# Turning part of the second stage's input with VectorE and DRAM instead of TensorE

## The chip, the cores and the metric

The kernel runs on one core of a Trainium2 chip. The metric is the device time of one execution in microseconds (us). The time before the change is the median of three runs.

## What is computed

The reference is a decoder trunk of two layers over 512 tokens and a model width of 2048, all in float32. The first layer is differential attention. Its normalised output is the input of the second stage: a shared projection to keys, values and forget gates, and then the second layer, forgetting attention. Cut to what matters here:

```python
x  = layer_norm(DN_ALPHA * x + gate * y, ln_g[0], ln_b[0])      # end of layer 0; (512, 2048)
hk = x * (1.0 + scale) + shift                                   # scale and shift per feature
k, v, zf = split(hk @ w_kv)                                      # shared keys, values, gate logits
...
h  = x * (1.0 + scale_b) + shift_b                               # the second layer's own modulation
q, g = split(h @ w_q)
```

## The kernel before

A product of float32 matrices is made of three matmuls: each operand is split into a high part, rounded to the type that TensorE reads fast, and a low part, the rest. TensorE multiplies high by high, high by low and low by high (`products`, L174 to L176). Weights come by DMA into `wst` (four buffers, L76), ScalarE makes the high part `whi` (L94) and VectorE the low part `wlo` (L95), with three buffers each.

TensorE contracts over partitions, so the activations `Hh` and `Hl` have features on partitions and tokens along the row: 16 tiles of 128 features by 512 tokens. The layer norm needs the other layout. Its result `n` is one tile of 128 partitions with four row blocks b of 128 tokens, each 2048 features wide; `norm_a(b)` writes it (the first 1024 features by ScalarE, L1072; the rest by VectorE, L1073) and stores it to `n_dram` for later use (L1074). It runs when row block b has been through the last quarter of the first layer's output projection, so block 3 is ready last.

`build_half(s, half)`, L1076 to L1097, turns one unit: features 256 s to 256 s + 255 (two tiles, kt = 2s and 2s + 1) of the tokens 256 half to 256 half + 255 (two row blocks). TensorE makes four transposes of 128x128 through the identity into a PSUM bank (L1084). For each of the two tiles ScalarE applies scale and shift twice, to `htmp2` in float32 (L1092) and to the high part `Hh` (L1093), and VectorE subtracts for the low part `Hl` (L1094). Last, VectorE copies the turned tokens back into the place of `n` that they came from (L1097); from there `build_h` (L1118 to L1124) makes the second layer's `Hh` and `Hl` some 250 us later, one VectorE instruction of 512 columns for each of 16 tiles and a split.

There are 16 units. The loop at L1188 uses them in the order of `lag`:

```python
lag = [(0, 0), (0, 1), (0, 2), (0, 3), (1, 0), (1, 1), (1, 2)]
for s in range(4, KT // 2):
    lag += [(0, s), (1, s - 1)]
lag.append((1, KT // 2 - 1))
```

Each entry is (half, s). An iteration makes the first 512 value columns for the two row blocks of its half and the two tiles of its s: twelve matmuls of 512 columns. Two units are built ahead of the loop, in the tail of the output projection; every iteration but the third builds the next one, so the unit of iteration i + 1 is built in iteration i. The weights of one s serve both halves and stay in `held` in between; those of s = 3 lie in a tile of another pool, the others in the three buffers of `whi` and `wlo`.

All DMAs that the change touches are issued by SyncE (SP), whose queue also loads the weights (L47). The tile framework orders each engine's instructions by a simulated schedule, in which an instruction traced later may go first when its inputs are ready; `keep_in_program_order` holds one behind the instruction traced before it on its engine. In this loop the background stream that sums the modulation vectors (L393) does not run.

The kernel already turns other tiles by a trip through DRAM: the attention weights of both layers and the first layer's output (L760 and L768, L826 and L834, L1302 and L1310). A VectorE instruction turns every 32x32 block in itself, one DMA writes the result to DRAM, and four or eight DMAs of 32 partitions each read the blocks back in their new places.

## Time and profile before

| | |
|---|---|
| median of three runs | 1961.45 us (1961.02 to 1962.36) |
| the profiled execution | 1958.95 us |
| its span | 1957.2 us |
| mean granted TensorE clock over the span | 0.995 |
| busy: TensorE (PE), its weight loads, VectorE, ScalarE | 98%, 83%, 69%, 36% |
| transposes of n (L1084) | 64, from 983.3 to 1034.9 us |

Times in the profile are microseconds from the start of the span unless marked ns. PE is TensorE's matmul, PEld its weight load, DVE is VectorE, ACT ScalarE, SP the engine that issues most DMAs; a q behind a name is that engine's instruction sequencer. A line of the timeline has the start, the duration, the engine, the line of the kernel, the operation and what it writes and reads; x2 or x4 at its end says that it stands for so many instructions; in brackets is the idle time ahead of it and what ended that. A line of the stretches has the stretch, its length, the busy time of PE, PEld, DVE, ACT and POOL with their counts, the granted clock of TensorE as a share of full speed, the busy share of the DMA engines and GB/s.

### The profile page before, as it was taken

The numbers are of one execution on the slowest core, as the hardware profiler recorded it, in microseconds if no ns is written. First come the engines' busy times: TensorE is split into PE (matmuls) and PEld (weight loads), VectorE is DVE, ScalarE is ACT, GpSimd is POOL, SyncE is SP. The second block draws the span as 40 slices with busy tenths as digits, with TensorE's granted clock in tenths as the row PEclk, the third lists the DMA queues.
The fourth block names the chain that finished last, engine by engine and source line by source line (L and its number), as shares of the span: only waits on it lengthen the run. The fifth ranks groups of instructions, "written<-read, shape, count | busy, mean of one in ns | idle before, by whom it ended". The sixth has DMA issues, their size and how long they took to land.

```text
span 1957.2 us, 25652 instructions
## 1 busy us (share of the span) xinstructions
PE 1923.4 (98%) x8997; PEld 1619.0 (83%) x8997; DVE 1355.0 (69%) x2499; ACT 700.0 (36%) x1186; POOL 2.2 (0%) x10
## 2 busy tenths in 40 slices
PE   5999999999999999999999999999999999999997
PEld 4888888888888888888889998888888888888886
DVE  7886578767777778567675657776566666676657
ACT  2432444323332344531273223224343434353123
POOL 0000000000000000000000000000000000000000
PEclk8999999999999999999999999999999999999999
DMA  9983355676667675466537866775354555553622
GB/s 343 361 302 118 124 183 166 202 229 204 213 203 224 190 238 177 130 229 214 181 133 233 270 202 215 245 260 163 110 157 148 153 154 153 156 173 113 223 91 104
DMA packets 337582, 376.16 MB, mean 192 GB/s; under 512 B 67974, under 2 KB 247196, under 8 KB 336684
## 3 DMA queue, kind: packets, MB, share of 16 engines
q1 hardware_dynamic: 334496, 370.30, 58.8%
q10 hardware_dynamic: 2956, 4.22, 0.6%
q8 instruction: 71, 1.16, 0.2%
q14 instruction: 59, 0.48, 0.1%
HBM read 345.63 MB, written 28.79 MB: 191 GB/s over the span
## 4 chain that ended last, share of the span: by engine, by line
PE 93%; DVE 3%; DMA 1%; SPq 1%; issue 1%; ACT 0%; DVEq 0%; ACTq 0%
PE acc L174 28%; PE acc L175 28%; PE acc L176 28%; PE sc L174 2%; PE sc L175 2%; PE sc L176 2%; PE o L174 1%; PE o L175 1%; PE o L176 1%; DVE wlo L95 1%; SPq L473 0%; PE tr L541 0%; DMA nr<-n_dram 0%; DMA wst<-in_a_w_in_dram 0%; DVE sacc L500 0%
## 5 line engine op out<-in xcount | busy, mean ns | idle before, releaser
L94 ACT CAST whi<-wst 128x1024 fp32r<-128x1024 f32 (+3 forms) x330 | 333.5, 1011 | 736.5 <-PE acc L176 339.5
L95 DVE TENSOR_TENSOR wlo<-wst,whi 128x1024 fp32r<-128x1024 f32 (+3 forms) x330 | 385.7, 1171 | 280.6 <-ACT whi L94 267.9
L174 PE MATMUL acc<-whi,hh 128*128 128x512 f32 (+1 forms) x1296 | 494.0, 384 | 1.0 <-DVE ztmp L1007 1.0
L175 PE MATMUL acc<-wlo,hh 128*128 128x512 f32 (+1 forms) x1296 | 492.4, 380 | 0.3 <-DVE wlo L95 0.3
L176 PE MATMUL acc<-whi,hl 128*128 128x512 f32 (+1 forms) x1296 | 491.8, 380 | 0.0
L174 PE MATMUL acc<-hh,whi 128*128 128x512 f32 x1184 | 463.6, 392 | 0.0
L175 PE MATMUL acc<-hl,whi 128*128 128x512 f32 x1184 | 461.7, 390 | 0.0
L176 PE MATMUL acc<-hh,wlo 128*128 128x512 f32 x1184 | 460.9, 390 | 0.0
L174 PEld LDWEIGHTS acc<-whi,hh 128*128 128x128 f32 x1296 | 244.5, 189 | 41.0 <-DVE ztmp L1007 1.8
L176 PEld LDWEIGHTS acc<-whi,hl 128*128 128x128 f32 x1296 | 243.2, 188 | 41.7
L175 PEld LDWEIGHTS acc<-wlo,hh 128*128 128x128 f32 x1296 | 243.4, 188 | 38.9 <-DVE wlo L95 0.7
L393 DVE SCALAR_TENSOR_TENSOR macc<-ms,cact,macc 128x512 f32<-128x512 f32 x307 | 229.2, 747 | 56.3 <-DMA ms<-in_w_mod_dram 38.4
L176 PEld LDWEIGHTS acc<-hh,wlo 128*128 128x128 f32 x1184 | 222.3, 188 | 47.7
L174 PEld LDWEIGHTS acc<-hh,whi 128*128 128x128 f32 x1184 | 222.5, 188 | 43.2 <-issue 0.3
L175 PEld LDWEIGHTS acc<-hl,whi 128*128 128x128 f32 x1184 | 222.5, 188 | 42.2
L500 DVE SCALAR_TENSOR_TENSOR sacc<-sms,cact,sacc 128x512 f32<-128x512 f32 (+1 forms) x127 | 89.5, 705 | 5.7 <-DMA sms<-in_w_mod_dram 2.0
L728 ACT ACTIVATE e<-e,mn 128x128 f32<-128x128 f32 (+3 forms) x64 | 36.0, 563 | 103.0 <-DVE mn L724 102.9
L1289 ACT ACTIVATE eb<-eb,mnb 128x128 f32<-128x128 f32 (+1 forms) x64 | 36.0, 563 | 88.8 <-DVE mnb L1286 88.6
L724 DVE CUSTOM_DVE_ANT_0 e<-sc,bias 128x128 f32<-128x128 f32 (+3 forms) x64 | 31.1, 486 | 25.2 <-PE sc L176 25.2
L1286 DVE CUSTOM_DVE_ANT_0 eb<-sc,biasb 128x128 f32<-128x128 f32 (+1 forms) x64 | 31.1, 486 | 23.0 <-PE sc L176 22.4
L393 DVE SCALAR_TENSOR_TENSOR macc<-msk,cact,macc 128x512 f32<-128x512 f32 x53 | 39.7, 749 | 1.0
L1280 DVE SCALAR_TENSOR_TENSOR biasb<-nfb,F,mask 128x128 f32<-128x128 f32 (+1 forms) x64 | 34.6, 542 | 0.6
(264 smaller groups left out, 1714.9 us busy)
## 6 DMA issues: line engine op xcount, KB each, us to landing
wst<-in_a_w_in_dram SPq DMA_DIRECT2D x240, 256.0 KB, 3.8
ms<-in_w_mod_dram SPq DMA_DIRECT2D x136, 256.0 KB, 3.8
ms<-in_kv_w_mod_dram SPq DMA_DIRECT2D x64, 512.0 KB, 4.4
wst<-in_b_w_in_dram SPq DMA_DIRECT2D x128, 256.0 KB, 2.8
sms<-in_w_mod_dram SPq DMA_DIRECT2D x56, 512.0 KB, 6.8
wst<-in_kv_w_dram SPq DMA_DIRECT2D x40, 512.0 KB, 3.8
ms<-in_w_mod_dram SPq DMA_DIRECT2D x32, 512.0 KB, 4.2
wst<-in_a_w_out_dram SPq DMA_DIRECT2D x32, 512.0 KB, 4.2
```

Source lines behind the costliest of these rows:

```text
L94: self.nc.scalar.copy(hi[:, :, :w], st[:, :, :w])
L95: self.nc.vector.tensor_tensor(lo[:, :, :w], st[:, :, :w], hi[:, :, :w].bitcast(F32), op=ALU.subtract)
L174: PE.matmul(dst, lhs[0], rhs[0], start=start, stop=False)
L175: PE.matmul(dst, lhs[0], rhs[1], start=False, stop=False)
L176: PE.matmul(dst, lhs[1], rhs[0], start=False, stop=stop)
L393: ins = V.scalar_tensor_tensor(acc, w, cact[:, kt : kt + 1], acc, op0=ALU.mult, op1=ALU.add)
L500: V.scalar_tensor_tensor(acc, w, sc, acc, op0=ALU.mult, op1=ALU.add)
L724: V.tensor_tensor_reduce(out=e[:, :w], in0=sc[:, :w], in1=st["bias"][:, (3 - i) * P :], scale=-1.0, scalar=3.0e38, op0=ALU.add, op1=ALU.mi ...
L728: S.activation(e[:, :w], e[:, :w], AF.Exp, bias=mn, scale=-1.0, accum_out=rs)
L1280: V.scalar_tensor_tensor(bias[:, :w], cur[hd, "nf"][:, :w], F[:, i, hd : hd + 1], mask[:, (3 - i) * P :], op0=ALU.add, op1=ALU.add)
L1286: V.tensor_tensor_reduce(out=e[:, :w], in0=sc[:, :w], in1=bias[:, :w], scale=-1.0, scalar=3.0e38, op0=ALU.add, op1=ALU.min, accum_out=mn)
L1289: S.activation(e[:, :w], e[:, :w], AF.Exp, bias=mn, scale=-1.0, accum_out=rs)
```

## The change

Twelve of the 16 units are no longer turned by TensorE: all eight of half 1, and s = 4 to 7 of half 0. They go in six pairs (s, s + 1). `turn_n` has VectorE turn the 32x32 blocks of a pair with four instructions of 256 columns into a tile `tn` (two buffers), each pinned behind the VectorE instruction traced before it, and one DMA writes the 512 KB to a DRAM tile (three buffers). `fetch_n` reads them back with eight DMAs of 32 partitions, in pieces of 256 bytes, over the place in `n` that they came from. `turns` and `back` say in which iteration of the loop either happens: the pair (s 0 and 1, half 1) is turned in iteration 0, fetched in iteration 1 and built in iterations 3 and 4.

For a turned unit `build_half` has no transposes, no PSUM bank and no copy back. ScalarE reads the fetched `n` in SBUF instead; a row block of it now holds one tile's 256 tokens with its 32-token groups interleaved, and the access pattern of `place_n` puts them in order. `build_h` reads the same pattern, in two instructions of 256 columns for each tile instead of one of 512.

```diff
+    turned_n = {}
+    def turn_n(s, half):
+        pool, n, _ = zp
+        t = pool.tile([P, 2, 2, 256], F32, name="tn", tag="tn", bufs=2)
+        for u in range(2):
+            for q in range(2):
+                c0 = (2 * (s + u) + q) * P
+                src = n[:, 2 * half : 2 * half + 2, c0 : c0 + P].rearrange("p b (j c) -> p b j c", c=32)
+                tc.keep_in_program_order(V.transpose(t[:, q, u, :].rearrange("p (j b c) -> p b j c", b=2, c=32), src))
+        turned_n[s, half] = turned_n[s + 1, half] = dram.tile([2, 2, P, 256], F32, name="turned_n", tag="turned_n", bufs=3)
+        nc.sync.dma_start(turned_n[s, half].rearrange("q u p e -> p q u e"), t)
+
+    def fetch_n(s, half):
+        src = turned_n[s, half].rearrange("q u (a r) (j e) -> q j r (u a) e", a=4, j=4)
+        for j in range(4):
+            for q in range(2):
+                to = zp[1][32 * j : 32 * j + 32, 2 * half + q, 2 * s * P : (2 * s + 4) * P]
+                nc.sync.dma_start(to.rearrange("p (x e) -> p x e", e=64), src[q, j])
+
+    def place_n(s, half, q):
+        return zp[1][:, 2 * half + q, 2 * s * P : (2 * s + 2) * P].rearrange("p (a b c) -> p b a c", b=2, c=32)

     def build_half(s, half):
         pool, n, _ = zp
+        hs = slice(256 * half, 256 * half + 256)
+        if turned(s, half):
+            for q in range(2):
+                kt = 2 * s + q
+                if half == 0:
+                    new_h(kt)
+                tmp = pool.tile([P, 256], F32, name="htmp2", tag="htmp2", bufs=2)
+                src = place_n(s, half, q)
+                sc, sh = ab["kv"][0][:, kt : kt + 1], ab["kv"][1][:, kt : kt + 1]
+                for dst in (tmp, Hh[kt][:, hs]):
+                    S.activation(dst.rearrange("p (b a c) -> p b a c", b=2, c=32), src, AF.Identity, scale=sc, bias=sh)
+                V.tensor_tensor(Hl[kt][:, hs], tmp, Hh[kt][:, hs].bitcast(F32), op=ALU.subtract)
+            return
         px = sc_bank()
...
     def build_h(kts, ab):
...
-            nt = n[:, :, kt * P : (kt + 1) * P]
-            V.tensor_scalar(tmp.rearrange("p (b t) -> p b t", t=P), nt, ab[0][:, kt : kt + 1], ab[1][:, kt : kt + 1], op0=ALU.mult, op1=ALU.add)
+            s, q = divmod(kt, 2)
+            for half in range(2):
+                to = tmp[:, 256 * half : 256 * half + 256]
+                if turned(s, half):
+                    to, nt = to.rearrange("p (b a c) -> p b a c", b=2, c=32), place_n(s, half, q)
+                else:
+                    to, nt = to.rearrange("p (b t) -> p b t", t=P), n[:, 2 * half : 2 * half + 2, kt * P : (kt + 1) * P]
+                V.tensor_scalar(to, nt, ab[0][:, kt : kt + 1], ab[1][:, kt : kt + 1], op0=ALU.mult, op1=ALU.add)
...
+    turns = {0: (0, 1), 1: (2, 1), 2: (4, 0), 3: (6, 0), 5: (4, 1), 8: (6, 1)}
+    back = {1: (0, 1), 2: (2, 1), 3: (4, 0), 5: (6, 0), 7: (4, 1), 10: (6, 1)}
     for i, (half, s) in enumerate(lag):
+        if i in back:
+            fetch_n(*back[i])
+        if i in turns:
+            turn_n(*turns[i])
         if i != 2:
             build_next()
```

More of the change, by code (lines that the diff above doesn't have):

```diff
@@ L1074, in norm_a, with turned @@
         nc.sync.dma_start(n_dram[b * P : (b + 1) * P, :], n[:, b, :])
+    turned_n = {}
[15 more added lines that the diff above has]
+                nc.sync.dma_start(to.rearrange("p (x e) -> p x e", e=64), src[q, j])
+    def turned(s, half):
+        return (s, half) in turned_n
+    def place_n(s, half, q):
+        return zp[1][:, 2 * half + q, 2 * s * P : (2 * s + 2) * P].rearrange("p (a b c) -> p b a c", b=2, c=32)
     def build_half(s, half):
         pool, n, _ = zp
+        hs = slice(256 * half, 256 * half + 256)
[11 more added lines that the diff above has]
+            return
         px = sc_bank()
-        hs = slice(256 * half, 256 * half + 256)
         for q in range(2):
```

## The prediction

> **What bounds the kernel now.** I read the page first, for the engine that carries the time, then the PE timeline of the stage that the change touches, then what the stage's PE work waits for.

> ```profile
> span 1957.2 us, 25652 instructions
> PE 1923.4 (98%) x8997; PEld 1619.0 (83%) x8997; DVE 1355.0 (69%) x2499; ACT 700.0 (36%) x1186; POOL 2.2 (0%) x10
> PE 93%; DVE 3%; DMA 1%; SPq 1%; issue 1%; ACT 0%; DVEq 0%; ACTq 0%
> ```

> The span is PE work from end to end: 98% busy, and 93% of the chain that ended last. So time that PE saves or loses in a stage reaches the end one for one, unless another wait takes its place. The profiled execution took 1958.95 us around this span; the median of the runs shown is 1961.45, 2.5 us above. I make the sum as a difference inside the profiled execution and add it to the median. A measurement of this kernel tells about 0.2%, 3.9 us, from no change.

> The stage is the loop over `lag`: sixteen iterations of twelve matmuls each. The PE timeline, start and duration first:

> ```profile
> 994.03 0.40 PE L174 MATMUL acc<-whi,hh 128*128 128x512 f32 x1
> ...
> 998.60 0.39 PE L176 MATMUL acc<-whi,hl 128*128 128x512 f32 x1
> 998.84 0.27 PE L1084 MATMUL sc<-ident,n 128*128 128x128 f32 x1
> ...
> 1000.15 0.55 PE L1084 MATMUL sc<-ident,n 128*128 128x128 f32 x3
> ...
> 1015.27 0.60 PE L1084 MATMUL sc<-ident,n 128*128 128x128 f32 x4
> ...
> 1018.48 0.60 PE L1084 MATMUL sc<-ident,n 128*128 128x128 f32 x4
> ```

> From 994.03 to 998.60 there are 21 matmuls, 20 steps: 0.2285 us each. An iteration without transposes is therefore 12 x 0.2285 = 2.74 us. With a unit's four transposes it is 1018.48 - 1015.27 = 3.21. So four transposes cost PE 0.47 us, not the sum of their durations.

> At 998.84 the first transpose of unit (half 1, s 0) goes out, and the other three only at 1000.15. The reason, and the end of the stage:

> ```profile
> 998.85 1.25 ACT L1072 ACTIVATE n<-n,mr,lrstd 128x1024 f32<-128x1024 f32 x1 [3.30 <-DVE mr L1071]
> PEld sc L1084 <- ACT n L1072: 0.6, 1, 0.6
> 1040.69 0.59 ACT L1139 COPY vt<-acc 128x512 f32<-128x512 f32 x1 [0.54 <-PE acc L176]
> 998.84:1040.70 41.86, 41.73 (x207) 34.05 (x206) 24.55 (x43) 31.52 (x59) 0.00 (x0) 1.00 0.26 86
> ```

> The fourth row block of n is normalised at 998.85 + 1.25 = 1000.10, by ACT. PE waits 0.6 us for it. At 1040.69 the last accumulator of the stage is read out. From 998.84, where iteration 3 begins, to there are 41.86 us with 13 iterations: 13 x 2.74 = 35.65 of products, and 6.2 of transposes and waits. That 6.2 us is all that the change can win, since units 0 to 3 keep their transposes.

> **The change part by part.**

> *Removed from PE:* 48 transposes in 12 units, 12 x 0.47 = 5.6 us; with the wait of 0.6 that is the 6.2 above, all of it on the path.

> *Vector and scalar work.* Rows of the groups by shape (count, then busy us and mean ns):

> ```profile
> L1300 DVE STREAM_TRANSPOSE tb<-eb 128x256 f32<-128x256 f32 x14 | 6.2, 444 | 0.4
> L1097 DVE COPY n<-sc 128x512 f32<-128x512 f32 x16 | 10.8, 683 | 0.0
> L1092 ACT ACTIVATE htmp<-sc,mod_b,mod_a 128x256 f32<-128x256 f32 x32 | 18.1, 565 | 5.5 <-PE sc L1084 5.1 <-DVE hl L1094 0.4
> L1123 DVE TENSOR_SCALAR htmp<-n,mod_a,mod_b 128x512 f32<-128x512 f32 x16 | 8.7, 543 | 0.3
> 1280.00:1350.00 70.00, 70.00 (x311) 57.68 (x310) 56.06 (x83) 24.50 (x32) 0.00 (x0) 1.00 0.62 208
> ```

> 24 VectorE transposes of 256 columns come in, 24 x 0.444 = 10.7 us; 12 copies go out, 12 x 0.683 = 8.2. DVE gains 2.5 us in a stage where it works 24.6 of 41.9: hidden under PE. ACT's 48 activations keep shape and number, at 565 ns, and now read SBUF. In `build_h` each 512-column instruction becomes two of 256: at most 16 x 0.543 = 8.7 us more, if halves cost as much as wholes, in a stretch where DVE works 56.1 of 70 and PE is busy all 70. Hidden too; with that cover gone it would cost those 8.7.

> *The trip through DRAM.* Per pair of units: one write of 512 KB, and eight reads of 64 KB on the same SP queue. A read waits on SP for the write to land, and behind it are queued the next write and the weight loads (L47); the loads run stages ahead. The rows (KB, then median us from issue to landing), and SP's timeline:

> ```profile
> n_dram<-n SPq DMA_DIRECT2D x4, 1024.0 KB, 4.3
> turned<-tb SPq DMA_DIRECT2D x14, 256.0 KB, 2.0
> turned<-e SPq DMA_DIRECT2D x5, 256.0 KB, 4.5
> pTl<-turned SPq DMA_DIRECT2D x56, 64.0 KB, 2.2
> e<-turned SPq DMA_DIRECT2D x20, 64.0 KB, 4.6
> 785.71 3.86 SPq L834 DMA_DIRECT2D ogT<-turned_og  x8
> 1000.12 0.34 SPq L1074 DMA_DIRECT2D n_dram<-n  x1
> ```

> The first pair is (half 1, s 0 and 1), needed by iteration 4, the one after the 998.84 iteration. Its clock starts at 1000.10, because each transpose reads row blocks 2 and 3 together, and the pinned order puts it behind the norm:

> 1. Four transposes, 4 x 0.444 = 1.8: 1001.9.
> 2. The write. Bounds 2.0 and 4.5, by the two 256 KB rows. I take 4.0, near the upper, because the 1 MB store of n goes out at 1000.12 on the same queue ahead of it, and by its own 4.3 lands at 1004.4; the reads overwrite n and must wait for that store as well. 1005.9.
> 3. The reads. Eight issues in 3.86 us are about 0.49 apart. The activations of q = 0 need the seventh: 6 x 0.49 = 2.9, 1008.8. Landing between 2.2 and 4.6; I take 2.2, from the calmer stage, as the background stream does not run here: 1011.0.
> 4. Two activations, the second making the high part: by the rows below 0.47 apart and 0.56 long, 1.0: 1012.0.

> ```profile
> 1015.90 0.56 ACT L1092 ACTIVATE htmp<-sc,mod_b,mod_a 128x256 f32<-128x256 f32 x1 [0.78 <-PE sc L1084]
> 1016.37 0.56 ACT L1093 ACTIVATE hh<-sc,mod_b,mod_a 128x256 fp32r<-128x256 f32 x1
> ```

> PE's cover for this ends at 998.84 + 2.74 = 1001.6, the end of iteration 3. Nothing can be pulled forward:

> ```profile
> 1005.78 1.05 ACT L94 CAST whi<-wst 128x1024 fp32r<-128x1024 f32 x1 [0.83 <-PE acc L176]
> ```

> This cast, the weights of s = 4, waits for PE to finish with s = 0, since `whi` has three buffers; so unit (0, 4) cannot go ahead of (1, 0). PE stands from 1001.6 to 1012.0: **10.4 us** where it stood under one. With the low ends (2.0, 2.2) it is 8.4; with the high ends (4.5, 4.6) about 13.3.

> *The later pairs.* Two iterations use a pair up in 5.5 us; SP needs eight issues and a write, about 4.4. If the writes go out ahead of the waiting reads, the second pair's seventh read is issued at 1005.9 + 3.9 + 2.9 = 1012.7, in place by 1015.9 with landing and activations, and iteration 6 asks for it at 1012.0 + 5.5 = 1017.5. I cost the later pairs at nothing, covered by 1.6 us.

> *The clock after the stall.* The first 60 us show what an idle PE does to its clock (third number from the end):

> ```profile
> 30.00:32.00 2.00, 1.11 (x4) 0.71 (x4) 0.98 (x3) 0.55 (x1) 0.00 (x0) 0.56 1.10 376
> 32.00:34.00 2.00, 0.99 (x2) 0.83 (x3) 0.34 (x1) 1.63 (x3) 0.00 (x0) 0.50 1.10 376
> 34.00:36.00 2.00, 2.00 (x6) 1.58 (x5) 1.93 (x4) 0.00 (x0) 0.00 (x0) 0.50 1.09 385
> 36.00:38.00 2.00, 2.00 (x8) 1.53 (x8) 1.93 (x3) 0.71 (x1) 0.00 (x0) 0.73 1.09 385
> 44.00:46.00 2.00, 2.00 (x6) 1.52 (x6) 0.83 (x3) 0.10 (x1) 0.00 (x0) 0.50 1.08 376
> 46.00:48.00 2.00, 2.00 (x10) 1.67 (x9) 2.00 (x4) 0.60 (x1) 0.00 (x0) 0.67 1.09 385
> ```

> Twice the granted clock fell to 0.50 when PE had little to do and came back only after some us of full work. What was lost: 2 x (0.44 + 0.50 + 0.50 + 0.27) = 3.4 us in the first fall, 2 x (0.50 + 0.33) = 1.7 in the second. A stall of 10 us should do the same; bounds 1.7 and 3.4, I take 2.6, the middle, having no row nearer to either. [...]

> *The sum.* 35.65 + 10.4 + 2.6 = 48.65 us against 41.86: **+6.8 us**. From the median, 1968.3; the profiled execution would be near 1965.8. With all low ends 35.65 + 8.4 + 1.7 = 45.75, +3.9; with all high ends 35.65 + 13.3 + 3.4 = 52.35, +10.5.

> **The rivals.**

> *The trip is covered (faster).* If iteration 4 finds its input in time, the 6.2 us are won: 1955.2. The point that decides is stall plus clock loss below 6.2. For it: the scheduler sets each engine's order anew, and could bring the norm of the fourth row block forward, where ACT today waits 3.30 us for DVE. Against it: even so, with the low ends, the trip is 1.8 + 2.0 + 2.9 + 2.2 + 1.0 = 9.9 us, and the input would have to be ready near 992, 8 us earlier.

> *Short trip, clock holds (no change that can be told).* Low ends and no fall of the clock: 35.65 + 8.4 = 44.05, +2.2: 1963.6. For it: the calm rows of 2.0 and 2.2 come from a stage with traffic of its own. Against it: a gap of 8 us, and the store of n ahead in the queue.

> *SP serves pair after pair (slower still).* If a pair's write stands behind the eight reads of the pair before, each pair takes a write's landing (3.0, between 2.0 and the 4.0 taken above) and eight issues, 3.0 + 3.9 = 6.9 us, against 5.5 that PE needs: 1.4 us late for each of five pairs, 7 more, +13.8: 1975.3. For it: `fetch_n` comes before `turn_n` in every iteration, and SP works in order. Against it: SP's order is the scheduler's, which today puts another tile's write straight behind four reads:

> ```profile
> 1414.23 2.95 SPq L1310 DMA_DIRECT2D pTl<-turned  x4
> 1417.22 0.43 SPq L1302 DMA_DIRECT2D turned<-tb  x1
> ```

> **How the numbers follow.** The forecast, +3.9 to +10.5, has 0.55; the SP rival 0.17; the short trip 0.17; the covered trip 0.11. Slower by over 0.2% is 0.55 + 0.17 = 0.72; within 0.2% is 0.17; faster 0.11. The range 1962.0 to 1975.0 leaves out the covered trip and the far end of the SP rival. The likeliest case's own range is 1965.3 to 1972.0.

> **What would show it.** Right: TensorE transposes of n from 64 to 16; a PE gap of 8 to 13 us about 1002 on the old axis, ended by an ACT activation that itself waited for the fetched n; a granted clock near 0.5 for some us behind it; iterations of 2.74 us after that, with no second gap. Wrong: PE passing 1002 without a gap, or a gap under 5 us; a gap before every second iteration would mean the SP rival; PE gaps in the 1280 to 1350 stretch would mean that the split `build_h` was not free.

## The result, and the profile after

| | before | after |
|---|---|---|
| median | 1961.02 us (1960.45 to 1962.36, 5 runs) | **1981.26 us** (1980.51 to 1985.5, 5 runs) |
| ratio, 95% interval | | **1.0107 (1.0093 to 1.0122)** |
| the profiled execution, its span | 1958.95, 1957.2 | 1985.5, 1983.7 |

The change costs 20.2 us. The forecast was 6.8 slower, 1962.0 to 1975.0: the sign held, the size did not.

The top of the page of the changed kernel, to be laid beside the page of before:

```profile
span 1983.7 us, 25652 instructions
PE 1928.7 (97%) x8949; PEld 1619.4 (82%) x8949; DVE 1358.8 (68%) x2527; ACT 701.5 (35%) x1186; POOL 2.2 (0%) x10
PE 90%; DVE 4%; DMA 3%; SPq 1%; ACT 1%; issue 1%; DVEq 0%; ACTq 0%
```

PE has 48 matmuls fewer (8949 against 8997): the transposes are gone. PE holds 90% of the last chain where it held 93%, and DMA 3% where it held 1%.

How much of this is the stage? ScalarE's weight casts (L94 and L89) are the same in both kernels, so they can be counted off. The 161st lies ahead of the stage, the 201st behind it. Their rows, before and then after:

```profile
934.46 1.05 ACT L94 CAST whi<-wst 128x1024 fp32r<-128x1024 f32 x1 [4.39 <-PE acc L176]
1121.68 0.84 ACT L94 CAST whi<-wst 128x776 fp32r<-128x776 f32 x1 [3.40 <-PE acc L176]
```
```profile
936.38 1.05 ACT L94 CAST whi<-wst 128x1024 fp32r<-128x1024 f32 x1 [4.39 <-PE acc L176]
1143.94 0.84 ACT L94 CAST whi<-wst 128x776 fp32r<-128x776 f32 x1 [3.40 <-PE acc L176]
```

From one to the other it was 187.22 us and is 207.56: **20.3 us more, all in this stage**. This difference is called the stage's change below; it leaves out that the profiled executions reach the stage up to 4 us apart (the 161st cast lies between 933.8 and 937.7 in the profiles shown below), and it agrees with the change of the medians here. (The profiled execution of after loses another 4 us near 1835, in the second output projection. Its time, 1985.5, is the highest of the five, and no other profile of the study lies more than 2.8 us above before in that stretch.)

PE's timeline of the changed kernel, only the matmuls ahead of which PE stood (in brackets the idle time and what ended it):

```profile
1013.57 0.80 PE L174 MATMUL acc<-whi,hh 128*128 128x512 f32 x1 [9.93 <-ACT hh L1120]
...
1024.10 0.50 PE L174 MATMUL acc<-whi,hh 128*128 128x512 f32 x1 [2.13 <-ACT hh L1120]
...
1025.57 0.51 PE L174 MATMUL acc<-whi,hh 128*128 128x512 f32 x1 [0.38 <-ACT hh L1120]
...
1031.61 0.50 PE L174 MATMUL acc<-whi,hh 128*128 128x512 f32 x1 [1.22 <-ACT hh L1120]
...
1044.18 0.79 PE L174 MATMUL acc<-whi,hh 128*128 128x512 f32 x1 [3.77 <-ACT hh L1120]
```

The first gap was forecast, the other three were not. Together they are 17.4 us. And the stretches of the same trace, cut where the granted clock changes (length, busy time of PE, PEld, DVE, ACT and POOL with counts, clock, DMA share, GB/s):

```profile
1003.65:1008.86 5.21, 0.00 (x0) 0.00 (x0) 2.48 (x8) 0.00 (x0) 0.00 (x0) 1.00 0.94 338
1008.86:1013.57 4.71, 0.00 (x0) 0.00 (x0) 1.53 (x6) 1.14 (x3) 0.00 (x0) 0.50 0.57 130
1013.57:1019.10 5.53, 5.53 (x13) 4.01 (x14) 1.69 (x4) 2.90 (x6) 0.00 (x0) 0.50 0.77 229
1019.10:1025.92 6.82, 4.31 (x18) 2.83 (x16) 3.15 (x5) 4.96 (x8) 0.00 (x0) 1.00 0.51 137
1025.92:1029.34 3.42, 3.42 (x10) 2.63 (x9) 1.39 (x5) 0.09 (x1) 0.00 (x0) 0.50 0.60 138
...
1042.99:1049.82 6.83, 5.64 (x13) 4.12 (x14) 2.55 (x6) 6.01 (x12) 0.00 (x0) 0.50 0.49 126
```

Three falls to 0.50. PE works 5.53, 3.42 and 5.64 us at half clock (a product takes 0.43 us from start to start there, 1016.49 to 1018.63, against 0.227) and loses about half of each: 2.8 + 1.7 + 2.8 = 7.3 us. With the gaps that is 24.7; the transposes saved 6.3 (the first experiment below); 18.4 of the 20.3 are so accounted for. Most of the other 1.9 us lies in the way of counting: from start to start of PE's matmuls, against the 0.227 us of its steady pace, the five waits take 18.4 us instead of 17.4 and the slow matmuls lose 7.9 instead of 7.3; so counted, 20.0 of the 20.3 are found.

Why gaps 2 to 4? ACT's timeline of the changed kernel:

```profile
1012.43 0.60 ACT L1120 ACTIVATE htmp<-n,mod_b,mod_a 128x256 f32<-128x256 f32 x1 [10.40 <-DMA n<-turned_n]
...
1019.28 1.05 ACT L94 CAST whi<-wst 128x1024 fp32r<-128x1024 f32 x1 [2.81 <-PE acc L176]
1022.00 1.04 ACT L94 CAST whi<-wst 128x1024 fp32r<-128x1024 f32 x1 [1.68 <-PE acc L176]
1022.95 0.60 ACT L1120 ACTIVATE htmp<-n,mod_b,mod_a 128x256 f32<-128x256 f32 x1
...
1029.52 1.05 ACT L94 CAST whi<-wst 128x1024 fp32r<-128x1024 f32 x1 [3.51 <-PE acc L176]
1030.47 0.60 ACT L1120 ACTIVATE htmp<-n,mod_b,mod_a 128x256 f32<-128x256 f32 x1
...
1043.04 0.60 ACT L1120 ACTIVATE htmp<-n,mod_b,mod_a 128x256 f32<-128x256 f32 x1 [6.94 <-DMA n<-turned_n]
```

At 1022.00 and 1029.52 a weight cast, which waits until PE has freed a buffer of `whi`, stands ahead of the activations of the next unit. PE frees the buffer with its last ready product and then has nothing until the cast (0.95) and two activations (1.0) are done. Those activations have no wait of their own: the tokens of the first had landed by about 1017.2, those of the second by 1027.5. At 1043.04 it is otherwise: the tokens themselves are late. SP's timeline tells why:

```profile
1003.52 1.67 SPq L1091 DMA_DIRECT2D turned_n<-tn  x2
1007.52 7.95 SPq L1098 DMA_DIRECT2D n<-turned_n  x16
1015.57 0.95 SPq L1091 DMA_DIRECT2D turned_n<-tn  x2
1021.61 0.37 SPq L47 DMA_DIRECT2D wst<-in_kv_w_dram  x1
1022.08 7.82 SPq L1098 DMA_DIRECT2D n<-turned_n  x16
1029.99 6.23 SPq L1091 DMA_DIRECT2D turned_n<-tn  x2
...
1036.86 8.54 SPq L1098 DMA_DIRECT2D n<-turned_n  x16
```

The 6.23 us at 1029.99 are two issues of under half a microsecond and a wait between them: the last write, of (half 1, s 6 and 7), waits for its four VectorE transposes, and the reads of (half 1, s 4 and 5), wanted first, stand behind it. Writes stand behind reads too: the two writes at 1015.57 had their tokens turned by 1010.5 and stood behind the sixteen reads of 1007.52, and the first write at 1029.99, turned by 1027.3, stood behind those of 1022.08. From 1016.5 to 1021.6 another sixteen reads stand behind a weight load that waits for a buffer; until 1018.6 they would have waited for their write to land in any case.

The costs that the forecast had estimated, from the DMA rows and the groups of after:

```profile
turned_n<-tn SPq DMA_DIRECT2D x6, 512.0 KB, 3.5
n<-turned_n SPq DMA_DIRECT2D x48, 64.0 KB, 2.1
L1089 DVE STREAM_TRANSPOSE tn<-n 128x256 f32<-128x256 f32 x24 | 8.4, 412 | 3.4 <-DMA turned_n<-tn 2.7 <-ACT n L1072 0.6
```

The write landed in 3.5 us (4.0 was taken), a read in 2.1 (2.2), a transpose took 412 ns (444). The first trip was mis-sized nowhere by more than half a microsecond.

### The profile page after: what moved, and what is told of

It reads as the page before. It is cut to its first block, busy times and chain, and to the rows that moved or that the text cites. A ratio compares the mean times of both kernels' runs of the same rounds, so it can differ in the third digit from the quotient of the medians.

```text
span 1983.7 us, 25652 instructions
## 1 busy us (share of the span) xinstructions
PE 1928.7 (97%) x8949; PEld 1619.4 (82%) x8949; DVE 1358.8 (68%) x2527; ACT 701.5 (35%) x1186; POOL 2.2 (0%) x10
## 4 chain that ended last, share of the span: by engine, by line
PE 90%; DVE 4%; DMA 3%; SPq 1%; ACT 1%; issue 1%; DVEq 0%; ACTq 0%
PE acc L174 27%; PE acc L175 26%; PE acc L176 26%; PE sc L174 2%; PE sc L175 2%; PE sc L176 2%; PE o L174 1%; PE o L175 1%; PE o L176 1%; DMA sms<-in_w_mod_dram 1%; DMA ms<-in_kv_w_mod_dram 1%; DVE wlo L95 1%; SPq L1098 1%; PE tr L541 0%; DMA nr<-n_dram 0%
## 5 line engine op out<-in xcount | busy, mean ns | idle before, releaser
L94 ACT CAST whi<-wst 128x1024 fp32r<-128x1024 f32 (+3 forms) x330 | 333.4, 1011 | 746.6 <-PE acc L176 360.3
L95 DVE TENSOR_TENSOR wlo<-wst,whi 128x1024 fp32r<-128x1024 f32 (+3 forms) x330 | 385.6, 1171 | 286.4 <-ACT whi L94 272.9
L174 PE MATMUL acc<-whi,hh 128*128 128x512 f32 (+1 forms) x1296 | 496.8, 386 | 20.7 <-ACT hh L1120 17.4
L176 PE MATMUL acc<-whi,hl 128*128 128x512 f32 (+1 forms) x1296 | 494.9, 382 | 0.0
L174 PE MATMUL acc<-hh,whi 128*128 128x512 f32 x1184 | 463.6, 392 | 0.3 <-DVE sg L696 0.3
L176 PE MATMUL acc<-hh,wlo 128*128 128x512 f32 x1184 | 460.9, 390 | 0.0
L174 PEld LDWEIGHTS acc<-whi,hh 128*128 128x128 f32 x1296 | 246.1, 190 | 65.1 <-ACT hh L1120 21.0
L176 PEld LDWEIGHTS acc<-whi,hl 128*128 128x128 f32 x1296 | 245.2, 189 | 43.2 <-DVE hl L1121 1.1
L176 PEld LDWEIGHTS acc<-hh,wlo 128*128 128x128 f32 x1184 | 222.3, 188 | 47.4
L174 PEld LDWEIGHTS acc<-hh,whi 128*128 128x128 f32 x1184 | 222.4, 188 | 44.0 <-issue 1.0
## 6 DMA issues: line engine op xcount, KB each, us to landing
wst<-in_a_w_in_dram SPq DMA_DIRECT2D x240, 256.0 KB, 3.7
ms<-in_w_mod_dram SPq DMA_DIRECT2D x136, 256.0 KB, 3.8
wst<-in_b_w_in_dram SPq DMA_DIRECT2D x128, 256.0 KB, 2.9
```

Of the source, the lines that this page charges most:

```text
L94: self.nc.scalar.copy(hi[:, :, :w], st[:, :, :w])
L95: self.nc.vector.tensor_tensor(lo[:, :, :w], st[:, :, :w], hi[:, :, :w].bitcast(F32), op=ALU.subtract)
L174: PE.matmul(dst, lhs[0], rhs[0], start=start, stop=False)
L176: PE.matmul(dst, lhs[1], rhs[0], start=False, stop=stop)
```

## The experiments

Each kernel is the changed one with the edit shown. "Stage" is the stage's change against before, from the two casts; the ratio is to before, as it ran on the same chip (medians 1959.88 to 1960.09 us; 1961.02 beside the change).

| | units turned by VectorE | stage | PE gaps over 1 us | median | ratio (95%) |
|---|---|---|---|---|---|
| the change | 12 | +20.3 | 9.9, 2.1, 1.2, 3.8 | 1981.26 | 1.0107 (1.0093 to 1.0122) |
| no trip | 12, not turned | -6.3 | none | 1955.59 | 0.9980 (0.9971 to 0.9989) |
| first pair on TensorE | 10 | +3.5 | 3.3, 1.2 | 1963.97 | 1.0021 (1.0012 to 1.0030) |
| spare matmuls | 12 | +17.8 | 1.5, 2.1, 1.2, 3.7 | 1981.28 | 1.0101 (1.0086 to 1.0116) |
| reads by GpSimd | 12 | +16.5 | 13.5, 2.1, 1.2 | 1978.10 | 1.0094 (1.0080 to 1.0107) |
| casts pinned | 12 | +13.2 | 10.2, 3.3 | 1974.95 | 1.0080 (1.0064 to 1.0095) |
| casts pinned, reads by GpSimd | 12 | +10.2 | 13.6 | 1971.51 | 1.0059 (1.0046 to 1.0073) |
| first pair on TensorE, casts pinned | 10 | +5.0 | 3.7, 1.3 | 1963.09 | 1.0018 (1.0009 to 1.0027) |
| eight | 8 | -0.3 | 1.7 | 1959.40 | 0.9997 (0.9988 to 1.0005) |
| eight, casts pinned | 8 | -0.1 | 1.7 | 1958.57 | 0.9995 (0.9986 to 1.0003) |
| eight, pinned, reads by GpSimd | 8 | +0.3 | 1.7 | 1959.99 | 0.9999 (0.9990 to 1.0008) |
| six, pinned, reads by GpSimd | 6 | -2.3 | none | **1957.81** | **0.9989 (0.9980 to 0.9998)** |
| six, nothing else | 6 | -0.5 | 1.2 | 1958.30 | 0.9991 (0.9982 to 1.0000) |

**No trip.** `turn_n` and `fetch_n` do nothing: the transposes of the 12 units are left out on both engines, and so are the write and the reads; the activations read `n` unturned.

> Leaves out, for the twelve units, TensorE's transposes and also VectorE's, the write and the reads: ScalarE reads n as it stands, so the products are made from tokens that were not turned. What remains of the change is ScalarE reading SBUF and the split instruction of build_h. Theory A (all that was lost lies in the trip through DRAM): the whole gain of the transposes is seen, 1961.0 - 6.2 = 1954.8. Theory B (reading SBUF in the interleaved pattern, or the split build_h, costs time by itself): 1958 or more, with PE gaps in this stage or in the stretch 1280 to 1350.

1955.59, stage -6.3. This is the ceiling of the change, and the 6.2 us of the forecast. PE has no gap in the stage, and the lead over before is the same 5.1 us at the casts ahead of and behind the stretch of `build_h` (the profiled execution began 1.2 late), so its split and the activations that read SBUF cost nothing. All the loss is the trips and what stands in their way. The medians lie 4.4 us apart (2.2 to 5.7 by the interval), not 6.3; where the other 1.9 go was not found.

**First pair on TensorE.**

```diff
-    turns = {0: (0, 1), 1: (2, 1), 2: (4, 0), 3: (6, 0), 5: (4, 1), 8: (6, 1)}
-    back = {1: (0, 1), 2: (2, 1), 3: (4, 0), 5: (6, 0), 7: (4, 1), 10: (6, 1)}
+    turns = {1: (2, 1), 2: (4, 0), 3: (6, 0), 5: (4, 1), 8: (6, 1)}
+    back = {2: (2, 1), 3: (4, 0), 5: (6, 0), 7: (4, 1), 10: (6, 1)}
```

> As the changed kernel, but the pair (s 0 and 1, half 1) stays with TensorE: ten units turned. Theory A (the first trip has no cover, the later ones are late because of the order on SP's queue): the gap of 9.9 us and the 2.7 us at half clock behind it go, 0.9 us of transposes come back, and the pair (s 2 and 3, half 1) becomes the first: about 1969, between 1966 and 1973. Theory C (each pair is late by itself, whichever is first): the first gap only moves to the next pair, with about 10 us: 1979 to 1982.

1963.97, below the 1966 to 1973 of theory A: two units fewer, and 17 of the 20 us are gone. The gap of 9.9 is a matter of the first pair alone, but a gap of 3.3 opens at the next pair, whose trip now is the first. The last gap, of 3.8, has shrunk to 0.2, which theory A did not expect.

**Spare matmuls.** PE is kept busy in the first gap with 38 matmuls whose result nobody reads.

```diff
+        if i == 4:
+            spare = tr_bank()
+            for _ in range(38):
+                tc.keep_in_program_order(PE.matmul(spare, Hh[0][:, 0:P], held[3][0][0], start=True, stop=True))
```

> As the changed kernel, with 38 matmuls of 512 columns into a spare PSUM bank in the first gap; their result is not used. Theory A (part of the loss is the clock that falls in the gap): the first products behind the gap run at full clock, 2.4 to 2.7 us are won, 1978.7. Rival (the gap costs only its own length): 1981.3.

Stretches of this kernel:

```profile
1000.00:1010.00 10.00, 10.00 (x46) 8.26 (x45) 6.45 (x22) 1.25 (x1) 0.00 (x0) 1.00 0.73 272
1010.00:1020.00 10.00, 8.00 (x34) 5.95 (x33) 3.42 (x10) 5.11 (x9) 0.00 (x0) 1.00 0.69 184
1020.00:1030.00 10.00, 7.38 (x23) 4.79 (x22) 4.70 (x9) 5.27 (x9) 0.00 (x0) 0.83 0.64 161
```

The first fall of the clock is gone (1.00 through 1020), the other two come, the last of them 3.4 us long instead of 6.8. The stage is 2.5 us shorter than with the change, but some 1.1 of that belongs to the shorter last fall (1.7 lost instead of 2.8), so this does not measure the first fall by itself. The medians, 1981.28 and 1981.26, do not show it: four runs from 1976.69 to 1981.66 cannot settle 2.5 us. What the clock costs rests on the traces, not on this time.

**Reads by GpSimd.** The 48 reads go to a queue that has nothing else in it (`nc.gpsimd.dma_start` in `fetch_n`).

> As the changed kernel, with the 48 reads issued by GpSimd instead of SP; writes and weight loads stay on SP. Theory A (the later pairs are late because reads, writes and weight loads stand in each other's way on SP): the three later gaps (2.1 + 1.2 + 3.8 us) and two clock falls (1.7 + 2.9) go, if GpSimd issues a read in about the same time: 1969.6; the first gap stays near 10 us. Theory D (the reads, in pieces of 256 bytes, are slow by themselves, or eight issues in a row are the limit): the gaps stay, 1980 or more.

1978.10, between the two theories. Of the four gaps only the last goes. Gaps 2 and 3 stay as they were, 2.13 and 1.21: the weight load that held SP's reads until 1021.6 was not what PE waited for, as I had held it to be. The first gap grows to 13.5. GpSimd needs 0.58 us for an issue (40 reads in 23.17 us, the row of the kernel after the next) where SP needs 0.50 (16 in 7.95), and its reads land in 2.6 us where SP's took 2.1. For the seventh read of the first pair, the one that the high part waits for, this is worth more than the medians say: behind the norm it goes out 1.4 us later than SP's and lands in 4.1 us instead of 1.9, together the 3.6. Two writes of later pairs, which on SP stood behind the reads, now go out among them, at 1006.7 and 1008.2; that these slow the landing was not tested apart. The last gap is gone, and not because PE came later: the seventh read of (half 1, s 4 and 5) landed 31 us behind the norm of row block 3, and in the changed kernel PE began to stand for it 38 us behind that norm. SP's order made that gap.

**Casts pinned.** A weight cast may not go ahead of the activations traced before it. (Three lines more: the kernel's L94 is L95 in the pinned kernels, and every later line is moved by 3.)

```diff
-            self.nc.scalar.copy(hi[:, :, :w], st[:, :, :w])
+            cast = self.nc.scalar.copy(hi[:, :, :w], st[:, :, :w])
+            if self.pin:
+                self.pin(cast)
...
+    ws.pin = tc.keep_in_program_order        # ahead of the loop; None behind it
```

> The changed kernel with one edit: the casts of the weights (L94, ScalarE) are held in the order of the program within the loop, so that the activations of a unit go ahead of the casts traced after them. Theory A (ScalarE's order made gaps 2 and 3: a cast that waits for TensorE to free a weight buffer stands ahead of activations whose data have landed, and TensorE waits for those activations): the gaps 2.13 + 0.38 and 1.22 and the fall of the clock behind the first of them (1.7) go, 5.4 us, so about 1975.9 (1974.0 to 1977.5); the first gap of 9.9 and the last of 3.8 stay. Rival B (the fetched tokens of the pairs s = 2, 3 and s = 4, 5 landed too late, in whatever order ScalarE works): the gaps stay and the time is 1980 to 1982.5. Rival C (the casts become late for TensorE instead): a gap of about 1 us at matmuls that wait for whi, 1977 to 1981.

PE's timeline of this kernel (idle times over 1 us):

```profile
1011.38 0.80 PE L177 MATMUL acc<-whi,hh 128*128 128x512 f32 x1 [10.16 <-ACT hh L1123]
...
1034.79 0.50 PE L177 MATMUL acc<-whi,hh 128*128 128x512 f32 x1 [3.31 <-ACT hh L1123]
```

1974.95, 6.3 us below the change where 5.4 was expected. Gaps 2 and 3 and the fall of the clock behind them are gone; the first and the last stay. So ScalarE's order is shown to be the cause of these two. Of the last, SP's rows tell what is left:

```profile
1016.02 7.76 SPq L1101 DMA_DIRECT2D n<-turned_n  x16
1023.88 0.40 SPq L1094 DMA_DIRECT2D turned_n<-tn  x1
...
1027.84 4.50 SPq L1101 DMA_DIRECT2D n<-turned_n  x8
```

The tokens that PE then waits for, of (half 1, s 4 and 5), are turned by VectorE from 1017.21 to 1018.63, but their write stands until 1023.88 behind the sixteen reads of the two pairs before. It lands at 1027.2, and their own reads follow 0.7 us later, behind the last pair's write. What ScalarE's order did stands in the timeline of the changed kernel: ready activations stand behind a cast that waits, for all of the 1.68 us at 1022.00 and for the last 2.0 of the 3.51 at 1029.52.

**Casts pinned and reads by GpSimd, together.**

> The changed kernel (12 units) with both orders taken out: the casts of the weights held in program order, and the 48 reads issued by GpSimd. Theory A (the first trip is one loss; everything behind it is the order of ScalarE and of SyncE): only the first gap is left, 13.5 us because GpSimd issues a read every 0.58, with one fall of the clock. The reads on GpSimd alone gave 1978.1 and lost 2.13 + 0.38 + 1.21 to ScalarE's order and 1.7 to the clock behind it; without these 5.4, 1972.7 (1971.0 to 1974.5). Rival B (the later pairs are late in themselves): at least one gap above 1 us behind the first, 1975 to 1978.

PE's only wait of this kernel in the stage, and GpSimd's reads:

```profile
1016.58 0.80 PE L177 MATMUL acc<-whi,hh 128*128 128x512 f32 x1 [13.62 <-ACT hh L1123]
```
```profile
1007.51 23.17 POOL L1101 DMA_DIRECT2D n<-turned_n  x40 [845.10 <-DMA turned_n<-tn]
```

1971.51, within what theory A gave. With both orders out, no pair behind the first makes PE stand: the two queues made the later pairs late. That the later trips fit under PE's work, as the forecast had it, is shown for the second to the fourth pair, by the casts pinned alone, with a first gap of 10.2 us. For the fifth, (half 1, s 4 and 5), it is not: here its seventh read lands 31.8 us behind the norm of row block 3, and the activations take 1.1 more; with the casts pinned alone PE asked for them 31.8 behind its norm. GpSimd's reads would have left a gap of some 1 us there (an estimate from these rows); the longer first gap covered it.

**First pair on TensorE, casts pinned.**

> Ten of 16 units turned by VectorE (the pair s = 0, 1 of half 1 stays on TensorE) and the casts held in program order. With the first pair on TensorE alone the time was 1963.97 with gaps of 3.3 and 1.2 us. Theory A: the 1.2 was a cast standing ahead of activations and goes; the 3.3 is the trip of the pair (2, 1) itself, which lands 2.5 us after TensorE is free, and stays with its fall of the clock (1.7): 1962.8 (1961.8 to 1963.8). Rival B (data late): both stay, 1963.5 to 1964.5.

1963.09, not told apart from the 1963.97 without the pin. The gap of 3.3 stays (3.7), as both theories had it. The second, 1.2 without the pin, is 1.3, at another place: ACT now waits 3.66 us there for fetched tokens, whose sixteen reads SP began at 1016.1 and ended at 1025.3. Their two writes, turned by 1008.2, had stood until 1013.1 behind the sixteen reads before them. The time lies in theory A's range, but its gap of 1.2 did not simply go: with ScalarE's order mended, SP's came to light.

**Eight units, the last four s of each half.**

```diff
+    turns = {0: (4, 0), 1: (6, 0), 4: (4, 1), 6: (6, 1)}
+    back = {1: (4, 0), 3: (6, 0), 6: (4, 1), 9: (6, 1)}
```

> Eight of 16 units turned by VectorE: only s = 4 to 7 of both halves, turned in iterations 0, 1, 4 and 6 and fetched in 1, 3, 6 and 9; s = 0 to 3 on TensorE as before the change. Theory A (a trip costs nothing where at least three iterations of 2.73 us lie between the block norm and the use, and ScalarE isn't held up): 32 transposes fewer per TensorE, 8 x 0.47 = 3.8 us less than before, 1957.2 (1956.5 to 1958.2), no gap of TensorE above 1 us in the stage. Rival B (any pair that goes through DRAM in this loop meets a waiting cast or load and opens a gap with a fall of the clock): at least one gap of 1 to 3 us, 1959 to 1963.

1959.40, outside theory A's range and at the low end of B's. ACT's timeline of this kernel, where PE stands for 1.69 us:

```profile
1012.66 1.05 ACT L94 CAST whi<-wst 128x1024 fp32r<-128x1024 f32 x1 [1.67 <-PE acc L176]
1013.61 0.60 ACT L1120 ACTIVATE htmp<-n,mod_b,mod_a 128x256 f32<-128x256 f32 x1
```

Again a waiting cast ahead of ready activations. This time the clock did not fall. With two more gaps of 0.47 and 0.22 it took back most of what the transposes had saved.

**Eight units, casts pinned.**

> The eight units again, with the casts of the weights held in program order. Theory A: nothing is left for the order to repair where the trips are covered: within 1 us of the eight units alone, 1957.2 (1956.5 to 1958.2); if that kernel has a gap behind a waiting cast, this one has not and is faster by the gap's length. Rival C (casts that come later make TensorE wait for whi): slower than the eight units alone by 1 us or more.

1958.57. That gap is gone, as theory A had it, but the time is not lower by its length: one of 1.71 has come at the first pair of half 1, (s 4 and 5):

```profile
1005.41 7.78 SPq L1101 DMA_DIRECT2D n<-turned_n  x16
1013.29 0.95 SPq L1094 DMA_DIRECT2D turned_n<-tn  x2
...
1016.40 4.15 SPq L1101 DMA_DIRECT2D n<-turned_n  x8
```

Its tokens were turned by 1007.75; the write stood until 1013.29 behind sixteen reads and landed at 1016.39, and the reads went out at once. A weight load issued in between, at 1014.33, took 0.95 us of the time in which they waited for the write.

**Eight units, casts pinned, reads by GpSimd.**

> Eight units turned by VectorE (s = 4 to 7 of both halves), casts in program order and reads issued by GpSimd. Theory A: neither a cast nor a weight load stands ahead of activations or reads, so no gap above 0.5 us; 32 transposes of TensorE fewer are worth 8 x 0.36 to 0.47 = 2.9 to 3.8 us: 1956.8 (1956.0 to 1957.8). Rival D (the first pair is turned only behind the norm of row block 3 and has about 11 us until its use, which a trip of 12 to 14 us does not meet): one gap of 1 to 3 us, 1958 to 1960.

1959.99, rival D. PE's and ACT's rows of the gap:

```profile
1015.95 0.50 PE L177 MATMUL acc<-whi,hh 128*128 128x512 f32 x1 [1.65 <-ACT hh L1123]
```
```profile
1014.80 0.60 ACT L1123 ACTIVATE htmp<-n,mod_b,mod_a 128x256 f32<-128x256 f32 x1 [3.08 <-DMA n<-turned_n]
```

Neither order is left, and the first pair is late: it is turned behind VectorE's part of the norm of row block 3, whose store goes out at 1002.2, and PE asks for it at 1014.3. But it is not late by that distance alone. In the kernel before this one, where SP issues the reads, the same pair's seventh read went out 8.4 us behind the norm and landed in 2.2, and PE did not stand for it; here it goes out 9.8 us behind and lands in 2.7. The distance just fits SP's reads and does not fit GpSimd's.

**Six units, those used last; casts pinned, reads by GpSimd.**

```diff
+    turns = {3: (4, 1), 5: (6, 0), 7: (6, 1)}
+    back = {4: (4, 1), 6: (6, 0), 8: (6, 1)}
```

> Six units turned by VectorE, those used last: (4, 5) of half 1 turned in iteration 3, (6, 7) of half 0 in 5, (6, 7) of half 1 in 7; casts in program order, reads issued by GpSimd. Every trip now has at least 15 us from the norm to its use. Theory A: no gap above 0.5 us, and 24 transposes fewer are worth 6 x 0.36 to 0.47 = 2.2 to 2.8 us: 1957.6 (1957.0 to 1958.5), faster than before by more than its interval. Rival E (even covered trips cost about what they save, in VectorE's order or in waits for the low parts): 1959.5 to 1961.

Stretches of this kernel:

```profile
1000.00:1010.00 10.00, 9.84 (x49) 7.70 (x48) 7.11 (x21) 6.21 (x12) 1.67 (x3) 1.00 0.48 179
1010.00:1020.00 10.00, 10.00 (x52) 8.24 (x51) 8.04 (x18) 8.42 (x17) 7.67 (x14) 1.00 0.81 231
1020.00:1030.00 10.00, 10.00 (x46) 8.28 (x45) 6.10 (x11) 9.44 (x18) 4.59 (x8) 1.00 0.53 152
```

1957.81 and a stage of -2.3, as theory A had it: PE is busy at full clock, as before the change. With an interval of 0.9980 to 0.9998 it is the version that beats both kernels, if by 0.1%.

**The same six units, nothing else changed.**

> The six units of the kernel before this one with nothing else changed: casts in the scheduler's order, reads issued by SyncE. Those six units with the casts pinned and the reads on GpSimd gave 1957.81 (0.9989 of before). Theory A1 (distance alone is enough: with 15 us or more from norm to use, the scheduler has no late input to put a cast ahead of): no gap above 0.5 us, 1957.2 to 1958.5. Theory A2 (the order is needed as well: a cast that waits for TensorE, or reads behind a weight load that waits, still stand ahead of an input): one gap of 1 to 3 us, 1958.8 to 1961.

1958.30. PE still stands once, 1.23 us, behind a cast of ACT's:

```profile
1024.11 1.05 ACT L94 CAST whi<-wst 128x1024 fp32r<-128x1024 f32 x1 [3.33 <-PE acc L176]
1025.06 0.60 ACT L1120 ACTIVATE htmp<-n,mod_b,mod_a 128x256 f32<-128x256 f32 x1
```

By the time this is theory A1, by the gap A2. In the stage the two kernels of six units are 1.8 us apart, while their intervals overlap: by the medians distance alone brings 1.6 of the 2.1 us, by the stage 0.5 of the 2.3. How much of it is distance and how much order stays open.

## Why the prediction was right in sign and wrong in size

- *Gain of 6.2.* Right by the stage: 6.3 in the kernel without a trip; its medians show 4.4.
- *The first trip, 10.4.* Right: 9.93, by the steps forecast. The write and the reads landed where they were put.
- *The clock behind it, 2.6.* Near: 5.53 us at 0.50, 2.8 lost, in part by luck. The upper bound of 3.4 counted as lost also the time in which PE had nothing to do; by PE's busy time in the same rows (1.11, 0.99, 2.00 and 2.00 us) the first fall lost 2.5, and the middle of 1.7 and 2.5 would have been 2.1.
- *"The later pairs. ... I cost the later pairs at nothing, covered by 1.6 us."* **This is the step that failed.** Gaps 2 to 4 are 2.13 + 0.38 + 1.22 + 3.77 = 7.5 us, and two more falls of the clock 1.7 + 2.8: **12.0 us where nothing was put**. 6.8 and 12.0 make 18.8 of the 20.3. The data's own way was rightly reckoned for the second to the fourth pair, as the kernel with the casts pinned shows. What was missed is the way of an instruction: the sum followed the tokens from DMA to DMA and never asked what stands ahead of the activations on ScalarE (gaps 2 and 3, with 1.7 us of the clock), and for SP it asked only about the first two pairs, where the writes do go ahead of the reads, and not about the writes and reads of the pairs behind them (gap 4, with 2.8). The row that could have told it stood in the prediction: the cast at 1005.78, waiting 0.83 us for PE. It was used only to show that no later unit can be pulled forward.
- *The forecast's clause on the weight loads ("the loads run stages ahead")* was wrong: one stood 5 us at SP's head, and for the last 3.0 of these it held reads whose write had landed. PE did not wait for that: gap 3 stayed when the reads went to GpSimd.
- *The rival "SP serves pair after pair"* asked for a gap before every second iteration, because a pair's write would stand behind the reads of the pair before. That pattern did not come: SP put the first two writes ahead of sixteen reads, as the forecast had said, and made one gap of the three. But its mechanism was at work behind them: the next two writes stood behind those sixteen reads for 6.6 us and 5.1 us, the fifth behind the next sixteen for 2.7 us, and with the casts pinned the fifth for 5.3 us.
- *"Iterations of 2.74 us after that, with no second gap"* was the test that the trace failed. *`build_h`* cost nothing, as forecast.

## What to carry to other kernels

Work that is taken from a bound engine and given to a longer way pays only where the whole way fits between the input's birth and its use; count that distance first, and move only what has it (here six units of twelve, for 2 us). Then read, for each engine and queue on the new way, what stands ahead of the new instructions in their order and what that waits for: a cast that waits for the bound engine's buffer closes a ring with the input that the engine waits for (gaps of 2.13 and 1.22 us here), and a write that stands behind the reads of other tiles starts its own trip late (by 5.1 us here, from 1010.5 to 1015.57). In the changed kernel the four gaps were 17.4 us of idle time, three of them came with a fall of the clock to 0.50 that cost 7.3 more, and together they cost 24.7.

## What was not expected of the hardware

```profile
1017.25:1020.67 3.42, 3.42 (x9) 2.64 (x9) 2.65 (x5) 3.42 (x8) 3.01 (x6) 0.50 0.80 222
```
```profile
1012.70:1024.00 11.30, 9.61 (x43) 7.38 (x42) 5.16 (x9) 8.27 (x17) 0.00 (x0) 1.00 0.85 229
```

The first row is of the eight units with pinned casts and reads by GpSimd, the second of the eight units alone.
